# Recurrence hops of a hybrid RWKV/attention layer: the decayed old state is added on VectorE, the output products follow the next hop's first ones, and one woven product changes its place

## Chip, cores, metric

One core of a Trainium2 chip. The metric is the device time of one execution in microseconds, in three runs 1148.97 to 1151.8, median 1151.46. The engines: TensorE (PE in the profile; PEld are its weight loads), VectorE (DVE), ScalarE (ACT), GpSimd (POOL) and SyncE (SP, which issues transfers).

## What is computed

One layer of a diffusion backbone for 512 image tokens and 128 context tokens, 1024 wide: a bidirectional RWKV-7 recurrence (8 heads of 64) beside a neighbourhood attention, then a gated merge and a feed-forward part. The change concerns the recurrence. For every head and direction a 64x64 state s is carried over the tokens:

```python
def _wkv_step(s, inp):
    r, w, k, v, a, b = inp
    sa = jnp.einsum("bhvk,bhk->bhv", s, a)
    s = s * w[:, :, None, :] + sa[..., None] * b[:, :, None, :] + v[..., None] * k[:, :, None, :]
    return s, jnp.einsum("bhvk,bhk->bhv", s, r)

def _wkv_scan(s0, r, w, k, v, a, b, reverse):
    xs = tuple(jnp.moveaxis(t.astype(jnp.float32), 1, 0) for t in (r, w, k, v, a, b))
    s, ys = lax.scan(_wkv_step, s0.astype(jnp.float32), xs, reverse=reverse)
    return s, jnp.moveaxis(ys, 0, 1)
```

The scan runs forwards and backwards, and both outputs are added. Everything is fp32.

## The kernel before

The kernel does the scan in chunks of 64 tokens: eight chunks of image tokens (slots 0 to 7) and two of context tokens (slots 8 and 9). Inside a chunk all products are batched; only the state passes from chunk to chunk. Heads go in pairs: four rounds (`ct` 0 to 3), each with two heads `h`, head 0 in partitions 0 to 63 and head 1 in 64 to 127. A round has three parts: `main` builds a chunk's matrices, `inv` inverts its triangular ones (on VectorE), and `carry` passes the state along. Then the next round follows.

`carry` (from L1368) is a chain of eight hops `s`. In each hop both directions `d` and both heads go one chunk on, so a group of products is four matmuls of 64x64, or eight in hops 0 and 1, where the context chunks join. `ZV[:, l, h, :]` holds for a chunk `l` the state and the values, `Dt` the chunk's decay. A hop has three stages, each ended by a `yield`:

- A: the AG products (L1393) multiply the state; ScalarE copies them out as `x0` (L1396). Meanwhile TensorE does the identity products (L1405), which put a copy of the old state into the PSUM tile `pn`, and the R products (L1411), the state's own share of the output `Y`.
- B: the Rt products (L1420) on `x0`; ScalarE copies them into `ZV` (L1426, twice), over the old state.
- C: the TG0 products (L1433) are added to `pn`; VectorE multiplies `pn` by the decay into the next chunk's `ZV` (L1445, one instruction for each head, both directions at once). TensorE goes on with the TG1 products (L1450), the output's share of this hop. In hop 1 a copy of the context outputs ends the stage (L1453).

So the chain of a hop is: AG, copy, Rt, copies, TG0, update, next AG. TensorE would stand idle during every copy and update. `weave` fills these holes: at each `yield` it takes an entry of the plan `PRM["plan"]`, two numbers in the hops. The first says how many feature products from another part of the kernel (L223, 128x320 outputs in PSUM tiles `fl`) are put there, the second how many steps of the next round's preparation are taken (through `beside`, L1586 and below). "0.0 8.1 6.2" is one hop: none in stage A, eight in stage B, six in stage C. The `fl` tiles have two PSUM buffers. The first product of a new one waits for the engine that reads the tile before the last: ScalarE, or in round 3 VectorE (L1554, then L1556 on its result).

TensorE, VectorE, ScalarE and GpSimd execute their instructions in the order in which the schedule writes them. What stands behind a waiting instruction waits too. In round 3 VectorE also has L1579, for attention, in pairs between its other work. From round to round L552, L554, L742, L728 and L751 (the next round's preparation) and L1168 follow on VectorE; L1189 is the first product of the next `main`.

Of the kernel before, what the change touches and what calls it, by code (L numbers as in the profile page):

```python
# [7 lines left out]
F32 = mybir.dt.float32  # L8
F32R = mybir.dt.float32r
AF = mybir.ActivationFunctionType  # L10
ALU = mybir.AluOpType
# [3 lines left out]
P = 128  # L15
# [18 lines left out]
         "5.0.0 24.0.0 20.0.0 10.0.0 8.0.0 8.0.0 0.0.0"),  # L34
        ("10.0 1.0 12.1 0.2 0.0 8.1 6.2 0.0 8.1 6.2 0.0 8.1 12.2 0.0 8.1 6.2 0.0 8.1 6.2 0.0 7.1 5.2 "
         "0.0 9.1 6.2 6.0"),
        "22.0 2.0 2.0 2.0",
        ("0.0.0 0.0.0 2.0.1 10.0.0 1.0.0 2.1.1 2.1.1 2.1.1 2.1.1 1.1.1 10.0.0 3.1.0 2.0.0 2.0.0 2.0.0 "
         "2.1.0 2.1.0 10.0.0 2.1.0 2.1.0 2.1.0 2.1.0 2.1.0 2.1.0 12.0.0 2.0.0 2.0.0 2.0.0 2.0.0 2.0.0 "
         "5.0.0 24.0.0 20.0.0 10.0.0 8.0.0 8.0.0 0.0.0"),  # L40
        ("10.0 0.0 8.1 6.2 0.0 8.1 6.2 0.0 8.1 6.2 0.0 8.1 6.2 0.0 8.1 6.2 0.0 7.1 6.2 0.0 8.1 6.2 0.0 "
         "8.1 6.2 6.0"),
        "22.0 2.0 0.0 5.0",
        ("0.0.0 10.0.0 2.0.1 10.0.0 2.0.0 2.1.1 2.1.1 2.1.2 2.1.1 2.1.0 10.0.0 2.0.0 2.0.0 2.0.0 2.1.0 "
         "2.1.0 2.1.0 10.0.0 2.1.0 2.1.0 2.1.0 3.1.0 4.1.0 2.1.0 2.0.0 2.0.0 2.0.0 4.0.0 2.0.0 2.0.0 "
         "5.0.0 24.0.0 18.0.0 8.0.0 9.0.0 8.0.0 0.0.0"),
        ("10.0 0.0 8.1 14.2 0.0 8.1 6.2 0.0 8.1 6.2 0.0 0.1 6.2 0.0 8.1 6.2 0.0 8.1 6.2 0.0 8.1 6.2 "
         "0.0 8.1 6.2 6.0"),
        "27.2 0.0 0.0 5.0",
        ("0.0.0 16.1.0 8.1.1 9.0.0 2.1.0 8.1.1 13.1.1 0.1.1 0.1.1 0.1.1 0.1.0 6.1.0 6.1.0 6.1.0 6.1.0 "  # L50
         "6.1.0 6.1.0 7.1.0 6.0.0 6.0.0 6.0.0 6.0.0 6.0.0 6.0.0 7.0.0 6.0.0 6.0.0 6.0.0 6.0.0 6.0.0 "
         "6.0.0 6.0.0 11.0.0 8.0.0 8.0.0 2.0.0 0.0.0"),
        ("10.3 0.0 6.1 4.2 0.0 6.1 4.2 0.0 6.1 4.2 0.0 6.1 4.2 0.0 6.1 4.2 0.0 6.1 4.2 0.0 6.1 4.2 0.0 "
         "6.1 8.2 6.0"),
# [60 lines left out]
def body(ctx: ExitStack, tc: tile.TileContext, xs, xp, cols, consts, w_ada, b_row, w_rw, w_qkv,  # L115
# [26 lines left out]
    def nm(s):  # L142
        cn[0] += 1
        return f"{s}_{cn[0]}"
# [952 lines left out]
    with ExitStack() as s3:  # L1097
# [270 lines left out]
        def carry(ct, S, last):  # L1368
# [4 lines left out]
            Y = [wps(), wps()]  # L1373
            begun = []

# [10 lines left out]
            for s in range(8):  # L1386
# [4 lines left out]
                for g, (sl, d, l) in enumerate(items):  # L1391
                    for h in range(2):
                        pe.matmul(px[hrows[h], g * 64:g * 64 + 64], AG[:, l, h, :], ZV[:, l, h, :],  # L1393
                                  start=True, stop=True)
                x0 = sb.tile([P, 4, 64], F32, tag="x0", bufs=2, name=nm("x0"))
                act.copy(x0[:, :ng, :], V(px[:, :], [[64, ng], [1, 64]]))  # L1396
                todo = [(g, i) for g, i in enumerate(items) if i[0] != 7]
                if todo:

                    pn = wps()  # L1400
                    for g, (sl, d, l) in todo:
                        for h in range(2):
                            if sl != 8:
                                own = hrows[h]
                                pe.matmul(pn[own, g * 64:g * 64 + 64], idh(h), ZV[own, l, h, :],  # L1405
                                          start=once(pn, h), stop=False)
                for (sl, d, l) in items:
                    for h in range(2):
                        own = hrows[h]
                        if sl != 8:  # L1410
                            pe.matmul(V(Y[sl // 8][own, :], *ycol(sl, d)), ZV[own, l, h, :], R_[own, l, :],  # L1411
                                      start=once(Y[sl // 8], h), stop=False)
                if s == 7 and not PRM["lh"][ct]:
                    last()
# [20 lines left out]
                for g, (sl, d, l) in todo:  # L1435
                    if d == 0:
                        dl = line(sl, 1) - l
                        if sl == 9:
                            dve.tensor_tensor(out=zf, in0=V(pn[:, :], [[64, 2], [1, 64]], 64 * g),
                                              in1=V(Dt[:, 0, :], [[dl, 2], [0, 64]], l), op=ALU.mult)  # L1440
                            sp.dma_start(o_st[ct], zf)
                            continue
                        for h in range(2):
                            own = hrows[h]
                            dve.tensor_tensor(out=V(ZV[own, l + 1, h, :], [[128 * dl, 2], [1, 64]]),  # L1445
                                              in0=V(pn[own, :], [[64, 2], [1, 64]], 64 * g),
                                              in1=V(Dt[own, 0, :], [[dl, 2], [0, 64]], l), op=ALU.mult)
                for (sl, d, l) in items:
                    for h in range(2):
                        pe.matmul(V(Y[sl // 8][hrows[h], :], *ycol(sl, d)), ZV[:, l, h, :], TG[:, l, h, 1, :],  # L1450
                                  start=once(Y[sl // 8], h), stop=sl in (7, 9) and d == 1)
                if s == 1:
                    act.copy(y[:, 512:640], Y[1][:, 0:128])  # L1453
                yield
# [698 lines left out]
```

## Time and profile before

| | before |
|---|---|
| three runs, us | 1151.8, 1148.97, 1151.46 |
| median | 1151.46 |
| the profiled execution | 1151.04 |
| its span | 1149.3 |
| granted TensorE clock, mean | 0.995 |
| the four `carry` parts, from first to last hop, us | 43.84, 44.10, 43.20, 31.60 |

The profiled execution's time is 1.7 us longer than its span; that much lies before the first and behind the last instruction recorded. In rows of the profile a line such as L1445 is a line of the kernel, `out<-in` names what is written and read, `128x64` are partitions and elements, and "x8" counts records. An fp32 matmul leaves two records, so "x8" are four matmuls. Times in a timeline are microseconds from the span's start. Waits are given as "idle before, and what ended it". A view by windows gives for each stretch its length and how long each engine was busy in it.

### The profile page before, as it was taken

Reading aid. Unit: us, or ns where it says so; the run is one execution under the profiler, and the core shown is the slowest. Engines: PE = TensorE matmul, PEld = TensorE weight load, DVE = VectorE, ACT = ScalarE, POOL = GpSimd, SP = SyncE. Lnnn points to the kernel's source line nnn. Section 1 sums busy time; section 2 is a strip of 40 time slices with the busy share of each in tenths; the row PEclk is TensorE's granted clock in tenths of the full one; section 3 lists DMA queues with packets and bytes.
Section 4 is the critical chain, followed back from the end, with each engine's and each line's share of the span. In section 5 each row is a group of like instructions: output and inputs, shape, how many; then the busy total and the mean of one; then the engine's idle time right before and its main releaser. Section 6 shows DMA issues by size and latency. Waiting matters only on the chain.

```text
span 1149.3 us, 26860 instructions
## 1 busy us (share of the span) xinstructions
PE 1117.0 (97%) x11160; PEld 990.9 (86%) x11160; DVE 777.8 (68%) x1641; ACT 533.7 (46%) x1052; POOL 195.1 (17%) x262
## 2 busy tenths in 40 slices
PE   6999999999999999999999999999999999999998
PEld 4688878799888888888898788999899989998997
DVE  4565465769558847936787846897478747874775
ACT  4444576665465665456443524654134413441340
POOL 1163244321101212120100421110101010101000
PEclk8999999999999999999999999999999999999999
DMA  9752677654433533343743872222212221232122
GB/s 340 261 113 91 199 277 236 198 153 125 107 75 86 148 85 93 96 119 86 254 122 105 265 213 72 92 93 93 91 56 92 94 90 55 92 97 88 55 91 94
DMA packets 60482, 149.16 MB, mean 130 GB/s; under 512 B 7460, under 2 KB 22436, under 8 KB 60360
## 3 DMA queue, kind: packets, MB, share of 16 engines
q1 hardware_dynamic: 54888, 131.16, 34.7%
q0 software_dynamic: 4032, 14.68, 6.5%
q10 hardware_dynamic: 1440, 1.59, 0.5%
q8 instruction: 88, 1.44, 0.5%
q14 instruction: 34, 0.28, 0.1%
HBM read 118.41 MB, written 14.32 MB: 115 GB/s over the span
## 4 chain that ended last, share of the span: by engine, by line
PE 74%; DVE 10%; issue 8%; ACT 4%; DMA 2%; POOL 1%; SPq 0%; ACTq 0%; DVEq 0%; POOLq 0%
PE acc L311 24%; PE f L1856 21%; PE fl L223 8%; PE mm L223 5%; PE psa L1044 1%; PE lg L959 1%; PE pt L988 1%; DVE RL L1321 1%; DVE pr L1317 1%; PE po L1006 1%; PE w L1420 1%; PE w L1393 1%; DMA o<-o_d 1%; PE w L1433 1%; DMA wlo<-wst 1%
## 5 line engine op out<-in xcount | busy, mean ns | idle before, releaser
L1856 PE MATMUL f<-t,whi 128*128 128x320 f32 x640 | 141.7, 310 | 0.2
L311 PE MATMUL acc<-whi,u 128*128 128x512 f32 (+1 forms) x448 | 136.1, 386 | 0.0
L1856 PE MATMUL f<-b,whi 128*128 128x320 f32 x608 | 135.0, 310 | 0.4 <-DVE b L212 0.4
L223 PE MATMUL fl<-h,whi 128*128 128x320 f32 x672 | 121.4, 321 | 0.0
L1856 PEld LDWEIGHTS f<-t,whi 128*128 128x128 f32 x640 | 106.8, 188 | 0.8 <-issue 0.4
L223 PEld LDWEIGHTS fl<-h,whi 128*128 128x128 f32 x672 | 102.1, 189 | 4.6
L192 ACT CAST whi<-wst 128x1024 fp32r<-128x1024 f32 (+1 forms) x77 | 79.3, 1033 | 52.2 <-PE acc L311 41.5
L1856 PEld LDWEIGHTS f<-b,whi 128*128 128x128 f32 x608 | 101.7, 188 | 1.1 <-issue 0.6
L1856 PE MATMUL f<-t,wlo 128*128 128x320 f32 x320 | 98.9, 309 | 0.0
L311 PEld LDWEIGHTS acc<-whi,u 128*128 128x128 f32 x448 | 83.5, 188 | 16.6
L1856 PE MATMUL f<-b,wlo 128*128 128x320 f32 x304 | 94.1, 309 | 0.0
L1909 ACT CAST whi<-ws 128x1024 fp32r<-128x1024 f32 x40 | 42.0, 1051 | 104.5 <-PE f L1856 45.6
L311 PE MATMUL acc<-wlo,u 128*128 128x512 f32 (+1 forms) x224 | 86.3, 385 | 0.0
L1923 POOL TENSOR_TENSOR ws<-wst 128x512 f32<-128x512 f32 x20 | 29.1, 1454 | 334.7 <-DVE wlo L1912 226.3
L195 DVE TENSOR_TENSOR wlo<-wst,whi 128x1024 fp32r<-128x1024 f32 (+2 forms) x57 | 60.1, 1066 | 30.6 <-ACT whi L192 30.0
L311 PE MATMUL acc<-whi,h 128*128 128x512 f32 x240 | 79.2, 404 | 0.8 <-DVE h L436 0.8
L1724 DVE SCALAR_TENSOR_TENSOR tt<-acc,G 128x512 f32<-128x512 f32 (+1 forms) x51 | 34.7, 680 | 59.0 <-PE acc L311 45.4
L223 PE MATMUL fl<-h,wlo 128*128 128x320 f32 x336 | 63.8, 322 | 0.0
L1909 ACT CAST whi<-wst 128x1024 fp32r<-128x1024 f32 (+1 forms) x48 | 41.3, 869 | 42.3 <-PE acc L311 25.1
L1856 PEld LDWEIGHTS f<-t,wlo 128*128 128x128 f32 x320 | 60.1, 188 | 0.0
L1912 DVE TENSOR_TENSOR wlo<-ws,whi 128x1024 fp32r<-128x1024 f32 x40 | 55.4, 1386 | 5.4 <-ACT whi L1909 5.4
L1445 DVE TENSOR_TENSOR ZV<-w,Dt 64x128 f32<-64x128 f32 x64 | 18.4, 288 | 58.5 <-PE w L1433 57.4
(342 smaller groups left out, 2533.2 us busy)
## 6 DMA issues: line engine op xcount, KB each, us to landing
wst<-in_w_dram SPq DMA_DIRECT2D x66, 512.0 KB
wst<-in_w_rw_dram SPq DMA_DIRECT2D x31, 512.0 KB
wlo<-wst POOLq DMA_DIRECT2D x28, 512.0 KB, 4.7
wa<-in_w_ada_dram SPq DMA_DIRECT2D x24, 512.0 KB
f<-in_w_ada_dram SPq DMA_DIRECT2D x16, 512.0 KB
wst<-in_w_qkv_dram SPq DMA_DIRECT2D x12, 512.0 KB
o<-o_d SPq DMA_DIRECT2D x14, 320.0 KB
x<-in_xs_dram SPq DMA_DIRECT2D x8, 512.0 KB
```

The source lines that it names most:

```text
L192: act.copy(hi[:, :n], st[:, :n])
L195: dve.tensor_tensor(out=lo[:, a:b], in0=st[:, a:b], in1=hi[:, a:b].bitcast(F32), op=ALU.subtract)
L223: pe.matmul(ps[:, :t1 - t0], w[:, a:a + 128], x[:, k0 + kt, t0:t1], start=n == 0, stop=n == 3 * nk - 1)
L311: pe.matmul(pss[i][:, a:b], lhs(x, kt, ts_), w[:, cs_], start=ki == 0 and n == 0, stop=ki == last and n == 2)
L959: pe.matmul(psl[:, hd, o_:o_ + n], qT[ft][rows, qs], x[rows, :], start=True, stop=True)
L988: pe.transpose(pst[:, c * 128:(c + 1) * 128], L[:, c * 128:(c + 1) * 128], ident)
L1445: dve.tensor_tensor(out=V(ZV[own, l + 1, h, :], [[128 * dl, 2], [1, 64]]), in0=V(pn[own, :], [[64, 2], [1, 64]], 64 * g), in1=V(Dt[own, 0, ...
L1724: dve.scalar_tensor_tensor(out=tt, in0=ps[:, a:b], scalar=c, in1=G[:, g, sl], op0=ALU.mult, op1=ALU.mult)
L1856: pe.matmul(ps[:, :H2], w_[:, c_], x_[:, kt, :], start=first and kt + n == 0, stop=last and kt == 3 and n == 2, skip_group_check=more)
L1909: act.copy(r[0][:, :width], src())
L1912: dve.tensor_tensor(out=r[1][:, :width], in0=src(), in1=r[0][:, :width].bitcast(F32), op=ALU.subtract)
L1923: eng_x(PRM["se"][i - 1]).tensor_tensor(out=o_, in0=x, in1=y, op=op)
```

## The change

In each hop that has a successor (slots 0 to 6) the identity products go. In their place VectorE computes `sd`, old state times decay, right behind the update that made this state (`decayed`, two instructions of 64x128 a hop; hop 0's stand behind its R products). The update is then `pn` times decay plus `sd`, for which a scalar from a pointer is needed: four `scalar_tensor_tensor` of 64x64 a hop (direction 0 head 0, direction 0 head 1, direction 1 head 0, direction 1 head 1) in place of two `tensor_tensor` of 64x128. Only slot 9 keeps its identity products. The TG1 products of a hop are written behind the AG products of the next (`ysum(back)`), those of hop 7 at its end; the copy of the context outputs goes to hop 2 with them. `x0` has one buffer for two. In the plan most hops have one product less in stage B and one more in stage C; the other numbers of the table are unchanged. The rows of rounds 0 and 3 before and after (rounds 1 and 2 are changed alike):

```diff
-        ("10.0 1.0 12.1 0.2 0.0 8.1 6.2 0.0 8.1 6.2 0.0 8.1 12.2 0.0 8.1 6.2 0.0 8.1 6.2 0.0 7.1 5.2 "
-         "0.0 9.1 6.2 6.0"),
+        ("10.0 1.0 11.1 1.2 0.0 7.1 7.2 0.0 7.1 7.2 0.0 8.1 12.2 0.0 7.1 7.2 0.0 7.1 7.2 0.0 6.1 6.2 "
+         "0.0 8.1 7.2 6.0"),
...
-        ("10.3 0.0 6.1 4.2 0.0 6.1 4.2 0.0 6.1 4.2 0.0 6.1 4.2 0.0 6.1 4.2 0.0 6.1 4.2 0.0 6.1 4.2 0.0 "
+        ("10.3 0.0 5.1 5.2 0.0 5.1 5.2 0.0 5.1 5.2 0.0 5.1 5.2 0.0 5.1 5.2 0.0 5.1 5.2 0.0 5.1 5.2 0.0 "
          "6.1 8.2 6.0"),
@@ -1371,7 +1371,22 @@
             S.y = y = out_t()
             zf = sb.tile([P, 2, 64], F32, tag="zf", bufs=1, name=nm("zf"))
             Y = [wps(), wps()]
-            begun = []
+            sd = sb.tile([P, 2, 64], F32, tag="sd", bufs=1, name=nm("sd"))
+            begun, back = [], []
+
+            def decayed(l):
+
+                for h in range(2):
+                    own = hrows[h]
+                    dve.tensor_tensor(out=sd[own, :, :], in0=V(ZV[own, l, h, :], [[128 * 12, 2], [1, 64]]),
+                                      in1=V(Dt[own, 0, :], [[12, 2], [0, 64]], l), op=ALU.mult)
+
+            def ysum(items):
+
+                for (sl, d, l) in items:
+                    for h in range(2):
+                        pe.matmul(V(Y[sl // 8][hrows[h], :], *ycol(sl, d)), ZV[:, l, h, :], TG[:, l, h, 1, :],
+                                  start=once(Y[sl // 8], h), stop=sl in (7, 9) and d == 1)
 
             def once(t, h):
                 first = not any(b is t and i == h for b, i in begun)
@@ -1392,15 +1407,19 @@
                     for h in range(2):
                         pe.matmul(px[hrows[h], g * 64:g * 64 + 64], AG[:, l, h, :], ZV[:, l, h, :],
                                   start=True, stop=True)
-                x0 = sb.tile([P, 4, 64], F32, tag="x0", bufs=2, name=nm("x0"))
+                x0 = sb.tile([P, 4, 64], F32, tag="x0", bufs=1, name=nm("x0"))
                 act.copy(x0[:, :ng, :], V(px[:, :], [[64, ng], [1, 64]]))
+                if back:
+                    ysum(back)
+                    if s == 2:
+                        act.copy(y[:, 512:640], Y[1][:, 0:128])
                 todo = [(g, i) for g, i in enumerate(items) if i[0] != 7]
                 if todo:
 
                     pn = wps()
                     for g, (sl, d, l) in todo:
                         for h in range(2):
-                            if sl != 8:
+                            if sl == 9:
                                 own = hrows[h]
                                 pe.matmul(pn[own, g * 64:g * 64 + 64], idh(h), ZV[own, l, h, :],
                                           start=once(pn, h), stop=False)
@@ -1410,6 +1429,8 @@
                         if sl != 8:
                             pe.matmul(V(Y[sl // 8][own, :], *ycol(sl, d)), ZV[own, l, h, :], R_[own, l, :],
                                       start=once(Y[sl // 8], h), stop=False)
+                if s == 0:
+                    decayed(0)
                 if s == 7 and not PRM["lh"][ct]:
                     last()
                 yield
@@ -1440,17 +1461,26 @@
                                               in1=V(Dt[:, 0, :], [[dl, 2], [0, 64]], l), op=ALU.mult)
                             sp.dma_start(o_st[ct], zf)
                             continue
+                        if sl < 8:
+                            for e in range(2):
+                                for h in range(2):
+                                    own = hrows[h]
+                                    dve.scalar_tensor_tensor(
+                                        out=ZV[own, l + 12 * e + 1, h, :],
+                                        in0=pn[own, (g + e) * 64:(g + e) * 64 + 64],
+                                        scalar=V(Dt[own, 0, :], [[1, 1]], l + 12 * e),
+                                        in1=sd[own, e, :], op0=ALU.mult, op1=ALU.add)
+                            continue
                         for h in range(2):
                             own = hrows[h]
                             dve.tensor_tensor(out=V(ZV[own, l + 1, h, :], [[128 * dl, 2], [1, 64]]),
                                               in0=V(pn[own, :], [[64, 2], [1, 64]], 64 * g),
                                               in1=V(Dt[own, 0, :], [[dl, 2], [0, 64]], l), op=ALU.mult)
-                for (sl, d, l) in items:
-                    for h in range(2):
-                        pe.matmul(V(Y[sl // 8][hrows[h], :], *ycol(sl, d)), ZV[:, l, h, :], TG[:, l, h, 1, :],
-                                  start=once(Y[sl // 8], h), stop=sl in (7, 9) and d == 1)
-                if s == 1:
-                    act.copy(y[:, 512:640], Y[1][:, 0:128])
+                if s < 6:
+                    decayed(s + 1)
+                back = items
+                if s == 7:
+                    ysum(items)
                 yield
             act.copy(y[:, 0:512], Y[0][:, 0:512])
```

In the changed kernel the lines have other numbers: AG L1408, TG1 L1388, R L1430, Rt L1441, TG0 L1454, `sd` L1381, the update L1468 (the context chunks' L1476), L1584 and L1586 for L1554 and L1556, L1609 for L1579.

TensorE in round 1, the last hop but one, from its AG products to those of hop 7, before (w are PSUM tiles, h the features that the woven products multiply; a bracket names the engines waited for):

```order
L1393 MATMUL w_5772<-ZV,AG 64x64 [waits DVE_49] x2
L1393 MATMUL w_5772<-ZV,AG 64x64 x2
L1405 MATMUL w_5779<-ZV,K 64x64 [waits PE_49]
L1405 MATMUL w_5779<-ZV,K 64x64 x3
L1411 MATMUL w_5320<-R__2901,ZV 64x64 x4
L1420 MATMUL w_5788<-x_836_5777,Rt 64x64 [waits Activation_49]
...
L1433 MATMUL w_5779<-ZV,TG 64x64 [waits Activation_49] x2
L1433 MATMUL w_5779<-ZV,TG 64x64 x2
L1450 MATMUL w_5320<-TG,ZV 64x64 x4
L223 MATMUL fl_5744<-h_90,wlo_5368 128x320 x2
L223 MATMUL fl_5744<-h_91,wlo_5368 128x320 x2
L223 MATMUL fl_5744<-h_92,wlo_5368 128x320 x2
```

and in the changed kernel:

```order
L1408 MATMUL w_5772<-ZV,AG 64x64 [waits DVE_49] x4
L1388 MATMUL w_5321<-TG,ZV 64x64 x4
L1430 MATMUL w_5321<-R__2901,ZV 64x64 x4
L1441 MATMUL w_5788<-x_838_5777,Rt 64x64 [waits Activation_49]
...
L1454 MATMUL w_5783<-ZV,TG 64x64 [waits Activation_49] x2
L1454 MATMUL w_5783<-ZV,TG 64x64 x2
L223 MATMUL fl_5744<-h_89,wlo_5394 128x320
L223 MATMUL fl_5744<-h_90,wlo_5394 128x320 x2
L223 MATMUL fl_5744<-h_91,wlo_5394 128x320 x2
L223 MATMUL fl_5744<-h_92,wlo_5394 128x320 x2
```

The identity products are gone, the output products of the hop before stand in their place, seven woven products instead of six lie behind TG0, and each AG product has a wait for VectorE of its own.

VectorE in round 3, hops 3 and 4, before (mx, mt: the reading of a feature tile; P, kk, bv, mt: L1579's tiles):

```order
L1445 TENSOR_TENSOR ZV<-w_8666,Dt_6879 64x2x64 x2
L1554 SCALAR_TENSOR_TENSOR mx_8293<-mx_8293,fl_8628 128x320
L1556 TENSOR_TENSOR mt_7728<-mt_7728,mx_8293 128x320
L1579 SCALAR_TENSOR_TENSOR P_1069_8133<-pre_8633,P_1069_8133 128x320 x2
L1554 SCALAR_TENSOR_TENSOR mx_8653<-mx_8653,fl_8683 128x320
L1556 TENSOR_TENSOR mt_7932<-mt_7932,mx_8653 128x320
L1445 TENSOR_TENSOR ZV<-w_8718,Dt_6879 64x2x64 x2
L1579 SCALAR_TENSOR_TENSOR kk_8283<-pre_8655,kk_8283 128x320 x2
```

and in the changed kernel:

```order
L1468 SCALAR_TENSOR_TENSOR ZV<-w_8672,Dt_6880,sd_8443 64x64 x4
L1381 TENSOR_TENSOR sd_8443<-ZV,Dt_6880 64x128 x2
L1584 SCALAR_TENSOR_TENSOR mx_8296<-mx_8296,fl_8630 128x320
L1586 TENSOR_TENSOR mt_7731<-mt_7731,mx_8296 128x320
L1609 SCALAR_TENSOR_TENSOR P_1072_8136<-pre_8634,P_1072_8136 128x320 x2
L1609 SCALAR_TENSOR_TENSOR kk_8286<-pre_8657,kk_8286 128x320 x2
L1468 SCALAR_TENSOR_TENSOR ZV<-w_8724,Dt_6880,sd_8443 64x64 x4
L1381 TENSOR_TENSOR sd_8443<-ZV,Dt_6880 64x128 x2
L1584 SCALAR_TENSOR_TENSOR mx_8655<-mx_8655,fl_8685 128x320
L1586 TENSOR_TENSOR mt_7935<-mt_7935,mx_8655 128x320
```

The reading of the second feature tile (fl_8683, now fl_8685) stood ahead of hop 4's update and stands behind it and behind the two `sd`; the pair for kk came ahead of it.

TensorE at the end of the same hop 4, before:

```order
L1433 MATMUL w_8718<-ZV,TG 64x64 [waits Activation_49] x2
L1433 MATMUL w_8718<-ZV,TG 64x64 x2
L1450 MATMUL w_8438<-TG,ZV 64x64 x4
L223 MATMUL fl_8734<-o_7943,wlo_8296 128x320 x2
L223 MATMUL fl_8734<-o_7944,wlo_8296 128x320
L223 MATMUL fl_8756<-o_7943,whi_8597 128x320 [waits DVE_49]
L1393 MATMUL w_8764<-ZV,AG 64x64 [waits DVE_49] x2
```

and in the changed kernel:

```order
L1454 MATMUL w_8724<-ZV,TG 64x64 [waits Activation_49] x2
L1454 MATMUL w_8724<-ZV,TG 64x64 x2
L223 MATMUL fl_8736<-o_7950,whi_8298 128x320
L223 MATMUL fl_8736<-o_7946,wlo_8299 128x320 x2
L223 MATMUL fl_8736<-o_7947,wlo_8299 128x320
L223 MATMUL fl_8758<-o_7946,whi_8594 128x320 [waits DVE_49]
L1408 MATMUL w_8766<-ZV,AG 64x64 [waits PE_49]
```

In both the last woven product ahead of AG is the first of a new feature tile and waits for VectorE's reading of the tile before the last, fl_8683 or fl_8685; what moved is that reading, on VectorE, as shown above.

More of the change, by code (lines that the diff above doesn't have):

```diff
@@ L40 @@
          "5.0.0 24.0.0 20.0.0 10.0.0 8.0.0 8.0.0 0.0.0"),
-        ("10.0 0.0 8.1 6.2 0.0 8.1 6.2 0.0 8.1 6.2 0.0 8.1 6.2 0.0 8.1 6.2 0.0 7.1 6.2 0.0 8.1 6.2 0.0 "
-         "8.1 6.2 6.0"),
+        ("10.0 0.0 7.1 7.2 0.0 7.1 7.2 0.0 7.1 7.2 0.0 7.1 7.2 0.0 7.1 7.2 0.0 6.1 7.2 0.0 7.1 7.2 0.0 "
+         "7.1 7.2 6.0"),
         "22.0 2.0 0.0 5.0",
@@ L46 @@
          "5.0.0 24.0.0 18.0.0 8.0.0 9.0.0 8.0.0 0.0.0"),
-        ("10.0 0.0 8.1 14.2 0.0 8.1 6.2 0.0 8.1 6.2 0.0 0.1 6.2 0.0 8.1 6.2 0.0 8.1 6.2 0.0 8.1 6.2 "
-         "0.0 8.1 6.2 6.0"),
+        ("10.0 0.0 8.1 14.2 0.0 7.1 7.2 0.0 7.1 7.2 0.0 0.1 6.2 0.0 7.1 7.2 0.0 7.1 7.2 0.0 7.1 7.2 "
+         "0.0 7.1 7.2 6.0"),
         "27.2 0.0 0.0 5.0",
```

## The prediction

> **What bounds the kernel now.** First the page's busy times, then the windows of the four rounds of the recurrence, then the timeline of one hop on TensorE and VectorE, then the chain of waits where one round passes into the next.
>
> ```profile
> PE 1117.0 (97%) x11160; PEld 990.9 (86%) x11160; DVE 777.8 (68%) x1641; ACT 533.7 (46%) x1052; POOL 195.1 (17%) x262
> ```
>
> TensorE (PE) is busy for 97% of the span, so an instruction taken from it is worth its time wherever nothing else ends later. VectorE (DVE) has 32% to spare on average, but averages hide stages. The windows (length, then busy time of PE, PEld, DVE, ACT, POOL) are rounds 0 to 3 from their first to their last hop, the stretch behind round 3, and the single hops 1, 2, 3, 4 and 5 of round 3, cut at the start of the state update:
>
> ```profile
> 298.86:342.70 43.84, 42.19 (x595) 36.64 (x595) 17.68 (x36) 28.09 (x72) 5.34 (x9) 1.00 0.32 78
> 393.90:438.00 44.10, 42.56 (x598) 37.01 (x597) 22.07 (x42) 27.60 (x72) 7.69 (x11) 1.00 0.30 83
> 492.20:535.40 43.20, 42.08 (x593) 36.85 (x593) 17.35 (x35) 25.87 (x70) 5.91 (x9) 1.00 0.38 99
> 598.40:630.00 31.60, 31.56 (x528) 26.83 (x527) 20.69 (x50) 10.95 (x35) 0.00 (x0) 1.00 0.40 120
> 630.00:720.00 90.00, 87.28 (x454) 72.90 (x453) 59.32 (x112) 39.09 (x71) 25.88 (x26) 1.00 0.59 180
> 607.41:611.13 3.72, 3.72 (x65) 3.13 (x60) 2.39 (x7) 2.01 (x6) 0.00 (x0) 1.00 0.15 45
> 611.13:614.85 3.72, 3.72 (x66) 3.13 (x60) 3.16 (x9) 0.79 (x3) 0.00 (x0) 1.00 0.69 204
> 614.85:618.57 3.72, 3.72 (x66) 3.13 (x60) 3.25 (x9) 0.79 (x3) 0.00 (x0) 1.00 0.48 146
> 618.57:622.29 3.72, 3.72 (x66) 3.13 (x60) 3.25 (x9) 1.62 (x4) 0.00 (x0) 1.00 0.05 19
> 622.29:626.01 3.72, 3.72 (x66) 3.13 (x60) 2.52 (x6) 0.79 (x3) 0.00 (x0) 1.00 0.62 165
> ```
>
> Rounds 0 to 2 leave TensorE idle 1.65, 1.54 and 1.12 us, 4.3 together; round 3 leaves it 0.04, and behind it 2.7 of 90 us. So what round 3 gains or loses passes to the end almost whole. In its hops TensorE is full and VectorE has only 0.47 to 1.33 us left of 3.72. That is the place to look. Hop 2's update and what TensorE does next, then VectorE in the same stretch (start, length of the group):
>
> ```profile
> 612.03 0.45 PE L1393 MATMUL w<-ZV,AG 128*64 128x64 f32 x8
> 612.41 0.45 PE L1405 MATMUL w<-ZV,K 64*64 64x64 f32 x8
> 612.69 0.40 PE L1411 MATMUL w<-R__2901,ZV 64*64 64x64 f32 x8
> 612.92 0.42 PE L1420 MATMUL w<-x,Rt 64*64 64x64 f32 x8
> 613.28 0.41 PE L223 MATMUL fl<-o,wlo 128*128 128x320 f32 x1
> ...
> 614.35 0.45 PE L1433 MATMUL w<-ZV,TG 128*64 128x64 f32 x8
> 614.63 0.40 PE L1450 MATMUL w<-TG,ZV 128*64 128x64 f32 x8
> 614.96 0.41 PE L223 MATMUL fl<-o,whi 128*128 128x320 f32 x1
> ...
> 615.75 0.28 PE L1393 MATMUL w<-ZV,AG 128*64 128x64 f32 x2
> ```
>
> ```profile
> 611.13 0.61 DVE L1445 TENSOR_TENSOR ZV<-w,Dt 64x128 f32<-64x128 f32 x2 [0.37 <-PE w L1433]
> 611.77 0.49 DVE L1554 SCALAR_TENSOR_TENSOR mx<-mx,fl 128x320 f32<-128x320 f32 x1
> ...
> 612.70 0.89 DVE L1579 SCALAR_TENSOR_TENSOR mt<-pre,mt 128x320 f32<-128x320 f32 x2
> 613.50 0.89 DVE L1579 SCALAR_TENSOR_TENSOR P<-pre,P 128x320 f32<-128x320 f32 x2
> 614.85 0.28 DVE L1445 TENSOR_TENSOR ZV<-w,Dt 64x128 f32<-64x128 f32 x1 [0.46 <-PE w L1433]
> ```
>
> Read off: the update (L1445) starts 0.50 us after the TG0 products (L1433, 614.35 to 614.85) and takes 0.61 for its pair; the AG products of the next hop follow at 615.75, 0.90 after the update's start, so the update is hidden by 0.29. Four woven products with the change of tile shape behind them take 0.79 (614.96 to 615.75), six 1.07 (613.28 to 614.35): 0.14 each, and 0.23 for the change.
>
> **The identity products removed.** From AG to R is 0.66 us with the identity group (612.03 to 612.69). In hop 7, which has none, it is 0.38:
>
> ```profile
> 530.59 0.45 PE L1393 MATMUL w<-ZV,AG 128*64 128x64 f32 x8
> 530.97 0.33 PE L1411 MATMUL w<-R__2901,ZV 64*64 64x64 f32 x4
> ```
>
> So a group costs at most 0.28, and at least the 0.23 of an equal group (R, 612.69 to 612.92). I take 0.25, 21 groups in rounds 0 to 2: -5.25 us. Hop 0 of rounds 1 and 2 weaves nothing ahead of Rt, and with no earlier products to move there the wait for the x0 copy takes the group's place: +0.5. Of the 4.3 us of idle TensorE in these rounds I count six waits for ACT's copies: what is saved ahead of such a wait is waited, 6 x 0.25 = +1.5.
>
> **The output products moved.** They go from behind TG0 to behind AG: the same instructions, so nothing by themselves. There they do for the x0 copy what the identity products did. But they leave the place where they covered the state update, and one woven product (0.14) is put there for 0.28 to 0.33 taken away.
>
> **The four pointer-scalar updates.** The trace has no such instruction of 64x64. Its neighbours:
>
> ```profile
> L684 DVE SCALAR_TENSOR_TENSOR kk<-kt__626,C,w x3: 340/340/342, 313.9 to 511.1; 128x128 f32<-128x128 f32 x3
> L682 DVE SCALAR_TENSOR_TENSOR kk<-kt__626,C,w x3: 746/746/747, 313.3 to 510.4; 128x512 f32<-128x512 f32 x3
> L1310 DVE SCALAR_TENSOR_TENSOR RL<-RL x24: 234/241/251, 284.1 to 585.9; 128x28 f32<-128x28 f32 x12, 128x29 f32<-128x29 f32 x8, 128x30 f32<-128x30 f32 x4
> L1445 DVE TENSOR_TENSOR ZV<-w,Dt 64x128 f32<-64x128 f32 x64 | 18.4, 288 | 58.5 <-PE w L1433 57.4
> ```
>
> From 512 to 128 columns it falls by 406 ns, 1.06 a column; 64 columns fewer than L684 gives 0.27. Bounds: 0.22 (L1445 less 64 columns) and 0.34 (L684 unchanged); 28 columns at 0.24 speak for the middle, so 0.28. L1445's pair, which changes between the partition halves, takes 0.61 for 2 x 0.288, while the L1579 pairs, which stay in one place, overlap (0.89 for 2 x 0.49). The new ones alternate halves each time: 0.31 apart, 1.24 for four, 0.63 more than now.
>
> [...]
>
> Consequence where seven products are now woven behind TG0: TensorE reaches AG 0.28 + 0.05 + 7 x 0.14 + 0.23 = 1.54 after TG0. The fourth update is ready at 0.50 + 1.24 + 0.05 = 1.79, and the fourth AG product starts some 0.2 after the first, so AG may start at 1.59. A wait of 0.05 if VectorE is free at that moment, 0.29 with updates of 0.34 (0.37 apart); with 0.28 between them, and pieces of 0.8 us of VectorE's own work that may be in front, I take 0.13 for some 15 such hops: +2.0 (0 to 4.4). With five woven (round 3) it is 1.26 against 1.59: AG now hangs on VectorE.
>
> **Where the update ends last already.** Chain of waits, rounds 0 to 1 and end of round 2:
>
> ```profile
> 336.89 0.28 DVE ZV L1445
> ...
> 337.54 0.76 DVE vp L552
> ...
> 344.17 0.73 DVE AG L1168
> ...
> 347.50 0.54 PE w L1189 x34
> ```
>
> ```profile
> 530.03 0.84 DVE f L742
> ...
> 530.96 0.65 ACT NK L721
> 531.61 0.16 ACT x L1396
> ...
> 531.81 0.45 PE w L1420 x8
> ```
>
> From the last update on VectorE works without a gap worth naming to the next round's first products; in round 2 L742 stands behind hop 6's update, and ACT's L721 and x0 copy, and with them Rt, wait for it. In each the update is 0.6 longer; I count three (the change from round 1 to 2 looks the same): +1.8.
>
> Rounds 0 to 2: -5.25 + 0.5 + 1.5 + 2.0 + 1.8 = +0.55.
>
> **The decayed state.** Two tensor-tensors of L1445's form a hop, 0.65 with their gaps, right behind the update in VectorE's written order: VectorE has 0.63 + 0.65 = 1.28 us more a hop. In rounds 0 to 2 it has 22 us or more idle of 43, and it is hidden (if not, up to 0.65 x 18 = 12 us; nothing there waits for sd itself but the next update and the copies over the old state, both over 1 us later). In round 3 the windows say otherwise: hop 2 has 3.16 + 1.28 = 4.44 against 3.72, +0.72. Hop 3 loses L1554 and L1556 (two of 0.49) to hop 4 and takes the kk pair (0.89) from it: about 3.25 - 0.98 + 0.89 + 1.28 = 4.44, +0.72. Hop 1 with 2.39 + 1.28 = 3.67 stays inside. TensorE's own hop is then AG at 1.59 and from AG to TG0 2.32 - 0.28 + 0.28 - 0.14 = 2.18, 3.77 together: +0.05 for each of hops 1, 5 and 6; hop 5's VectorE has 2.52 + 1.28 = 3.80, +0.1 with it; hop 0 has six updates, +0.1.
>
> **A wait that the new order makes.** In hop 4 of round 3 the last woven product ahead of AG opens a feature buffer and waits for the L1554 of the buffer two before. That stood ahead of hop 4's update; now it stands behind the four updates and the two decays, and the AG, output and R products of hop 5 are queued behind the waiting product on TensorE. From the update's start: 1.24 + 0.65 + 0.49 (L1554) + 0.05 + 0.14 + 0.23 = 2.80 to AG, where it was 0.90: +1.90, less 0.14 by which AG to the next update gets shorter (2.68 for 2.82): +1.76.
>
> Round 3: 0.72 + 0.72 + 1.76 + 0.3 = +3.5. The rest (one x0 buffer, whose reader is done a hop earlier; the output copy behind x0; L650 and L660 in other places of ACT's order) I put at 0 with 0.5 either way. The sum: 0.55 + 3.5 = +4.05, which is 1155.1 from the profiled execution's 1151.04; that lies 0.4 under the median 1151.46, so **1155.5** against the median.
>
> **Rivals.**
> *The chip hides VectorE's part.* If an update is 0.22 and the alternating ones overlap, so that four end within 0.9, the AG waits vanish, rounds pass at +0.3 and only TensorE's saving counts: 28 x 0.25 = -7.0, + 0.5 + 1.5 + 0.9 = -4.1, hop 4's wait shrunk into hops with room: 1147.4. For it: PE 97%. Against: L1445's pair does not overlap.
> *Gain and loss cancel.* At 0.22, 0.25 apart, four take 1.0: no wait in rounds 0 to 2 (-2.0), three passages +0.4 instead of 0.6 (-0.6), three late hops 0.24 shorter (-0.7): +0.75, 1152.2.
> *VectorE becomes the bound, at L684's price.* 0.34, 0.37 apart, 1.48 for four: 0.24 more on every hop, 15 x 0.24 + 3 x 0.24 + 6 x 0.24 = +5.8: about 1161. It decides from 0.31 on, where AG waits in rounds 0 to 2 as well. Against it: fewer columns than L684.
> That the change doesn't do what it says can be left out: the built order shows 112 products gone and the new updates in place.
>
> **How the numbers follow.** The forecast 0.52, its own range 1152.5 to 1158; hidden 0.20; cancelled 0.10; VectorE's bound 0.18. A measurement here tells 0.3%, 3.45 us, from none: faster is under 1148.0, slower over 1154.9. The forecast lies close to that edge, two thirds of it above: slower 0.18 + 0.34 = 0.52, same 0.10 + 0.18 = 0.28, faster 0.20. The range 1148 to 1160 leaves out the better half of the first rival and the worse half of the last.
>
> **What would show it.** Right: updates of 0.27 to 0.29, 0.31 apart; hops 2 and 3 of round 3 near 4.4 with TensorE waiting for VectorE ahead of AG; the hop 4 to 5 passage 1.5 to 2 us longer, with a woven product waiting there for the read that was L1554; rounds 0 to 2 within 1 us of before. Wrong: updates under 0.25 or overlapping, round 3's hops still 3.7, or rounds 0 to 2 shorter by 3 us and more, which would mean that TensorE's saving was not eaten by ACT.

## The result and the profile after

The changed kernel takes 1163.24 us in the median of six runs (1161.16 to 1165.57), the kernel before 1151.12 (six runs): a ratio of 1.011 with an interval of 1.0093 to 1.0127, slower by 12 us. The forecast was 1155.5 with a range up to 1160. It was right that the change makes the kernel slower; the size was wrong.

First the page's own lines for the changed kernel: busy times, and TensorE's instruction fetches (packets, MB, share of the DMA engines).

```profile
PE 1120.7 (96%) x10936; PEld 991.2 (85%) x10936; DVE 810.0 (70%) x1753; ACT 534.9 (46%) x1052; POOL 194.1 (17%) x262
...
q8 instruction: 86, 1.41, 0.5%
```

There are 224 TensorE records fewer (112 products), and TensorE is still busy for 3.7 us longer. So work was taken away and what is left takes longer. The starts of the AG products tell where: each round's first and its hop 7, read from the timelines of both kernels.

| stretch | before, us | after, us | difference |
|---|---|---|---|
| up to round 0 | 298.86 | 296.94 | -1.9 |
| hops of round 0 | 38.37 | 37.96 | -0.4 |
| between rounds 0 and 1 | 56.99 | 62.39 | +5.4 |
| hops of round 1 | 38.97 | 36.29 | -2.7 |
| between 1 and 2 | 59.17 | 58.94 | -0.2 |
| hops of round 2 | 38.23 | 39.17 | +0.9 |
| between 2 and 3 | 67.90 | 73.61 | +5.7 |
| hops of round 3 | 28.42 | 33.60 | +5.2 |
| the rest | 522.3 | 522.6 | +0.3 |

Round 3's hops lose 5.2 us where 3.5 were foretold. But 11 us lie between the rounds, in `main` and `inv`, which the change doesn't touch; round 1's hops, which start 3 us late, give some of it back. The windows of the two long stretches, before and then after (length, busy PE, PEld, DVE, ACT, POOL, then the granted clock):

```profile
337.20:394.20 57.00, 55.32 (x1082) 51.11 (x1082) 52.56 (x161) 33.35 (x66) 11.55 (x22) 1.00 0.44 112
...
530.60:598.50 67.90, 64.68 (x1149) 59.88 (x1148) 54.71 (x164) 33.40 (x68) 7.34 (x13) 1.00 0.50 166
```

```profile
334.90:397.30 62.40, 58.26 (x1092) 53.38 (x1092) 54.87 (x166) 33.34 (x66) 11.58 (x22) 0.97 0.41 105
...
531.70:605.30 73.60, 68.09 (x1155) 62.94 (x1155) 55.57 (x165) 33.52 (x68) 7.28 (x13) 0.95 0.47 153
```

The instructions are the same but for a handful, ACT and POOL are busy for as long. TensorE idles 4.1 and 5.5 us where it idled 1.7 and 3.2, and its clock is below 1.00. What it waits for in the whole kernel, by the view of waits (us in total, times, longest), before and after:

```profile
PE w L1208 <- issue: 1.5, 1, 1.5
...
PE w L1359 <- issue: 1.3, 1, 1.3
...
PE w L1259 <- issue: 0.4, 1, 0.4
...
PE w L1211 <- issue: 0.4, 1, 0.4
```

```profile
PE w L1211 <- issue: 4.1, 2, 2.6
PE fl L223 <- DVE mx L1584: 3.6, 3, 2.2
...
PE w L1359 <- issue: 1.4, 2, 0.7
...
PE w L1208 <- issue: 1.0, 1, 1.0
...
PE w L1189 <- issue: 0.6, 1, 0.6
```

"issue" is idle time for which the profile knows no releaser. It was 3.6 us, it is 7.3 (with one of 0.2 not shown). The longest, on TensorE's timeline, and the clock around it in windows of 2 us:

```profile
568.43 0.28 PE L1211 MATMUL w<-R__2901,f 64*64 64x64 f32 x3
571.29 0.21 PE L1211 MATMUL w<-R__2901,f 64*64 64x64 f32 x1 [2.58 <-issue]
```

```profile
568.00:570.00 2.00, 0.71 (x37) 0.58 (x28) 0.36 (x3) 0.00 (x0) 0.00 (x0) 1.00 0.26 95
570.00:572.00 2.00, 0.71 (x14) 0.61 (x14) 0.00 (x0) 0.00 (x0) 0.00 (x0) 1.00 0.02 3
572.00:574.00 2.00, 2.00 (x8) 1.77 (x7) 1.34 (x6) 0.78 (x2) 0.28 (x1) 0.55 0.03 8
574.00:576.00 2.00, 2.00 (x8) 1.61 (x8) 1.94 (x7) 0.15 (x1) 0.59 (x1) 0.59 0.00 0
576.00:578.00 2.00, 2.00 (x16) 2.00 (x15) 1.96 (x6) 0.74 (x2) 0.93 (x1) 1.00 0.42 159
```

In the middle of a burst of products of one kind TensorE stands for 2.58 us, all engines have next to nothing to do, and then the clock is at half for 3.4 us (in the trace's clock record from 572.21 to 575.62 us). In the kernel before, the same burst runs through. What differs is the instruction stream: the queue q8 of the page moves 1.44 MB in 88 packets before, 16 KB each, for 2 x 11160 TensorE records, about 64 bytes a record. A packet is thus 256 instructions, and one 64x64 fp32 product (two records and two weight loads) is four. Such a packet is called a block here. From 560 us to the end of the jam of data transfers (the queue's lines, before up to 566.5 us; after, 568.5 to 571.3):

```profile
q1 hardware_dynamic: 1243, 2.39, 96.9%
q8 instruction: 2, 0.03, 1.9%
```

```profile
q1 hardware_dynamic: 32, 0.06, 6.9%
q8 instruction: 1, 0.02, 2.2%
```

Before, two blocks are fetched while the data transfers have the DMA engines full. In the changed kernel the same view from 560 to 568.4 us lists no fetch at all; the next one lies within the stall (from 568.87 to 569.87 us). This gave the theory for the experiments (**fetch**): by 28 products a round, 112 instructions, the ends of the blocks move against the bursts of small products, and a block that ends in the wrong place is there too late. The rivals: the losses come from what the change does to other engines or to the order of loads (**work**); or they are chance.

Round 3, VectorE (hops 2 to 4) and TensorE (hop 4 to 5) in the changed kernel:

```profile
618.53 1.23 DVE L1468 SCALAR_TENSOR_TENSOR ZV<-w,Dt,sd 64x64 f32<-64x64 f32 x4 [0.20 <-PE w L1454]
619.79 0.61 DVE L1381 TENSOR_TENSOR sd<-ZV,Dt 64x128 f32<-64x128 f32 x2
...
622.96 1.22 DVE L1468 SCALAR_TENSOR_TENSOR ZV<-w,Dt,sd 64x64 f32<-64x64 f32 x4
...
627.39 1.19 DVE L1468 SCALAR_TENSOR_TENSOR ZV<-w,Dt,sd 64x64 f32<-64x64 f32 x4
628.61 0.61 DVE L1381 TENSOR_TENSOR sd<-ZV,Dt 64x128 f32<-64x128 f32 x2
629.25 0.49 DVE L1584 SCALAR_TENSOR_TENSOR mx<-mx,fl 128x320 f32<-128x320 f32 x1
```

```profile
629.79 0.41 PE L223 MATMUL fl<-o,whi 128*128 128x320 f32 x1 [2.23 <-DVE mx L1584]
630.13 0.65 PE L1408 MATMUL w<-ZV,AG 128*64 128x64 f32 x8
...
633.77 0.45 PE L1454 MATMUL w<-ZV,TG 128*64 128x64 f32 x8
```

VectorE goes from update to update in 4.43 us, with no pause of 0.15 us or more (618.53, 622.96, 627.39); the woven product of hop 4 waits 2.23 us for L1584; AG follows 2.74 us after the update's start. All that stood in the prediction. What did not: from AG to TG0 hop 5 takes 3.64 us (630.13 to 633.77) where 2.2 were foretold, at half clock (in the clock record from 630.24 to 633.65 us).

### The profile page after: what moved, and what is told of

Its sections match the earlier page's. It is cut to its first block, busy times and chain, and to the rows that moved or that the text cites. A ratio compares the mean times of both kernels' runs of the same rounds, so it can differ in the third digit from the quotient of the medians.

```text
span 1161.6 us, 26547 instructions
## 1 busy us (share of the span) xinstructions
PE 1120.7 (96%) x10936; PEld 991.2 (85%) x10936; DVE 810.0 (70%) x1753; ACT 534.9 (46%) x1052; POOL 194.1 (17%) x262
## 3 DMA queue, kind: packets, MB, share of 16 engines
q10 hardware_dynamic: 1440, 1.59, 0.5%
## 4 chain that ended last, share of the span: by engine, by line
PE 71%; DVE 11%; issue 9%; ACT 5%; DMA 3%; POOL 1%; SPq 0%; DVEq 0%; ACTq 0%; POOLq 0%
PE acc L311 24%; PE f L1886 21%; PE fl L223 9%; PE mm L223 5%; DVE RL L1321 1%; DVE pr L1317 1%; PE pt L988 1%; PE lg L959 1%; PE po L1006 1%; PE psa L1044 1%; DMA wa<-in_w_ada_dram 1%; PE w L1441 1%; DMA wlo<-wst 1%; PE w L1454 1%; PE w L1408 1%
## 5 line engine op out<-in xcount | busy, mean ns | idle before, releaser
L311 PE MATMUL acc<-whi,u 128*128 128x512 f32 (+1 forms) x448 | 136.0, 385 | 0.0
L311 PEld LDWEIGHTS acc<-whi,u 128*128 128x128 f32 x448 | 83.5, 188 | 16.7
L311 PE MATMUL acc<-wlo,u 128*128 128x512 f32 (+1 forms) x224 | 86.3, 385 | 0.0
L311 PE MATMUL acc<-whi,h 128*128 128x512 f32 x240 | 79.2, 404 | 0.4 <-DVE h L436 0.4
L1468 DVE SCALAR_TENSOR_TENSOR ZV<-w,Dt,sd 64x64 f32<-64x64 f32 x112 | 31.7, 283 | 42.9 <-PE w L1454 40.1
```

Of the source, the lines that this page charges most:

```text
L311: pe.matmul(pss[i][:, a:b], lhs(x, kt, ts_), w[:, cs_], start=ki == 0 and n == 0, stop=ki == last and n == 2)
L1468: dve.scalar_tensor_tensor(out=ZV[own, l + 12 * e + 1, h, :], in0=pn[own, (g + e) * 64:(g + e) * 64 + 64], scalar=V(Dt[own, 0, :], [[1, 1] ...
```

## The experiments

All are timed beside runs of the kernel before on the same chip (medians 1151 to 1152).

**More products, other place of the block ends.** At 16 us, where TensorE has pauses, idle products are put in, whose result is overwritten:

```diff
             ps = pp.tile([P, 512], F32, tag="tp", name=nm("xt"))
+            if i == 3 and q == 0:
+                for _ in range(N):
+                    pe.matmul(ps[0:64, 0:64], ident[0:64, 0:64], ident[0:64, 0:64], start=True, stop=True)
```

with N = 20 in the changed kernel, and 44, 64, 16 and 32 in the kernel before.

> The changed kernel with 20 idle TensorE products of 64x64 (80 instructions) put into TensorE's pause at 17 us, so that the stream up to round 3 is again as long as before's, counted modulo 256 instructions. Theory (fetch): the 2.58 us stall of TensorE at 568.7 us, for which the trace names no engine, is a block of 256 instructions fetched too late in a burst of small products; with the other phase it goes, and the half clock behind it too: 1163.2 - 2.6 - 1.5 = about 1159. Rival (work): the stall comes from what the change does to the other engines or to the order of the loads, and stays where it is: 1163 within 1.5.

> The kernel before with 44 such idle products (176 instructions, which is -80 modulo 256), so that it has the phase of the changed kernel at the start of round 3. Theory (fetch): a stall of 2 to 3 us appears near the L1211 products behind round 3's start, with 3.4 us of half clock behind it: 1151.1 + 4 = about 1155. Rival (work): no stall there, 1151 to 1152.5 (44 products cost at most 2.4 us if none of it is hidden).

> The kernel before with 64 idle TensorE products (256 instructions, one whole 16 KB block) at the place where 44 of them (176 instructions) gave 1163.5 us. Theory (fetch): only the place of the block ends counts; with a whole block every later block ends where it did before, so the stalls go again: 1151 to 1154 (64 products cost at most 3.5 us if none of it is hidden). Rival (work): idle products cost by themselves or by what they delay at the start: at least as much as 44 did, 1163 or more.

> The kernel before with 16 idle products (64 instructions, a quarter of a block). Theory (fetch): some phase between 0 (1151.3) and 176 (1163.5); the burst behind round 0 stalls as soon as its block ends later than its small products begin: anywhere from 1150 to 1163, with the sum of TensorE's unnamed stalls in the trace moving with the time. Rival (work, 16 products cost under 1 us): 1151 to 1152.

> The kernel before with 32 idle products (128 instructions, half a block). Theory (fetch): as with 16, another phase, 1151 to 1163, again with the unnamed stalls; were it a smooth cost of added work, it would lie between the times with 16 and 44.

| kernel | instructions added | modulo 256 | median, us | ratio to before | unnamed stalls of TensorE, us | half clock, us |
|---|---|---|---|---|---|---|
| before | 0 | 0 | 1151 | | 3.6 | 3.4 |
| pad_before16 | 64 | 64 | 1168.14 | 1.0144 (1.0124 to 1.0163) | 6.7 | 23.9 |
| pad_before32 | 128 | 128 | 1165.73 | 1.0111 (1.0087 to 1.0136) | 13.8 | 17.1 |
| pad_before | 176 | 176 | 1163.52 | 1.0111 (1.0096 to 1.0126) | 10.1 | 3.4 |
| pad_before64 | 256 | 0 | 1153.79 | 1.0018 (1.0006 to 1.0029) | 3.5 | 0 |

(The stalls are the sum of the lines "PE ... <- issue" of each profile; half clock is its time between 100 and 1140 us in the trace's clock record.) Sixteen idle products, which take TensorE 2.1 us in the trace, cost 17 us in a kernel that is otherwise unchanged; 64 of them, which take 7.7, cost 2.5 (that is 0.12 to 0.13 a product, where my expectations had 0.06). So it is not the work but the place modulo one block. The view of waits with 44 products, where L1214 is the line that was L1211:

```profile
PE w L1214 <- issue: 8.4, 6, 2.4
...
PE w L1262 <- issue: 1.7, 1, 1.7
```

With 44 the stretch between rounds 0 and 1 is 5.3 us longer, as in the changed kernel (5.4), though no instruction of the recurrence was edited, and the foretold stall is there: 2.37 us at 572.40, among the products where the changed kernel had 2.58.

The traces allow a direct count. Over all records of TensorE (products, weight loads and the sequencer's own, 22508 before) the 14 traces of the runs here have 75 unnamed stalls of 0.15 us or more, of 0.16 to 3.73. Every one of them begins behind a number of records that is 193 modulo 256 (the 2.58 us behind 14017), in the kernel before and move_only too. And each ends 1.2 to 1.6 us after a packet of q8 has landed, which in all 75 has the same number as the block: behind 256n + 193 records it is the n-th packet (the 54th ahead of the 2.58 us). A stall caused by other engines or by the order of loads would have no reason to keep to that count. So what TensorE waits for there is its next block of instructions.

So the theory holds in its main point. In its details my expectations missed: with 44 products 1155 was expected and 1163.5 came, with 16 at most 1163 and 1168 came; and pad_after, which should have come to 1159 because round 3 has before's phase again, took 1168.06 (1.0141, 1.0127 to 1.0155). There the stretch between rounds 2 and 3 does fall from +5.7 to +1.0 us against before, but the parts ahead of round 0 and behind round 3 got +6.0 and +2.7 (in the changed kernel -1.9 and +0.3). One pad can't set all the bursts, since the change moves each round's by another amount. How late a block will be I can't foretell; only that the same number of instructions modulo 256 gave nearly the same time (64 products here, and the last experiment). Is the sum of stalls alone the cost? With 16 products it grows by 3.1 us and the time by 17: 20 us more of half clock come behind, which by estimate cost half of that (three records of L587 that follow each other in 0.43 us before take 0.80 in r3_only at half clock), and later transfers (in that trace TensorE waits 3.6 us for one load of L311 that cost 0.6 before). With 44 there is no more half clock than before, the stalls make 6.5 of the 12 us, and the rest was not taken apart.

**The same number of instructions.** In the changed kernel the identity products are kept, into columns that nobody reads:

```diff
-                            if sl == 9:
+                            if sl != 8:
                                 own = hrows[h]
-                                pe.matmul(pn[own, g * 64:g * 64 + 64], idh(h), ZV[own, l, h, :],
+                                c = g * 64 + (256 if sl < 8 else 0)
+                                pe.matmul(pn[own, c:c + 64], idh(h), ZV[own, l, h, :],
```

> The changed kernel with the identity products kept as idle ones (in a part of the PSUM tile that nobody reads): all the work of the change plus the TensorE time that it was to save, but before's number of TensorE instructions at every place. Theory (fetch): the 11 us lost outside the recurrence's hops go (+5.4 ahead of round 1, +5.7 ahead of round 3), up to 7 us of TensorE time come back: 1154 to 1160, faster than the changed kernel although it does more. Rival (work): 1163 to 1170.

1160.18 us (1.0074, 1.0057 to 1.0091): 3 us faster than the changed kernel (1.011) with 112 products more. Its unnamed stalls are 2.7 us. The stretch between rounds 0 and 1 is +0.4 to before, for +5.4; between 2 and 3 +2.1, for +5.7. Its hops of round 3 lose 7.1 us, more than the changed kernel's 5.2, as TensorE has the idle products there as well. So with before's block ends most of the loss is in round 3.

**The change by rounds.** Each `if` of the change gets the round as a second condition, with the plan's rows to match; r012 has it in rounds 0 to 2, r3_only in round 3.

```diff
-                            if sl == 9:
+                            if sl == 9 or (ct in (0, 1, 2) and sl != 8):
...
-                if s < 6:
+                if s < 6 and ct not in (0, 1, 2):
                     decayed(s + 1)
```

> The change in rounds 0 to 2 alone; round 3 has the identity products, the two-headed update, the output products in their old place and its old row of the plan. If round 3's carry costs what the trace shows (5.2 us): 1163.2 - 5.2 = 1158.0, with TensorE's stall near 569 us still there, and 1152 plus what rounds 0 to 2 cost (about 1) if the stall is not a lasting part of the kernel. If the loss in round 3 came only from the lateness that it was handed: 1162.

> The change in round 3 alone; rounds 0 to 2 as before, so that the blocks lie as before up to round 3. Round 3's hops lose the 5.2 us that the changed kernel's trace shows there, nothing else: 1156.5 (1155 to 1158). If the stalls ahead of round 3 belong to what the change does in round 3: 1161 or more.

r3_only: 1156.66 (1.0042, 1.0026 to 1.0058), as foretold; its hops of round 3 are 4.24, 5.74, 4.05, 3.95, 6.84, 4.96 and 3.52 us, the changed kernel's to within 0.3. r012: 1160.13 (1.0084, 1.0068 to 1.01), 2 us above what I had expected; its round 3 has before's hops of 3.72 again, its rounds 0 to 2 the stretch +5.7 ahead of round 1 and +3.2 ahead of round 3. So rounds 0 to 2, where TensorE saves work and VectorE has room, cost 9 us alone. That the parts' 9.0 and 5.4 are more than the whole's 12.1 fits a cost that depends on the block ends of each kernel, but was not taken apart further.

**Round 3: the wait and what stands behind it.** r3_plan puts back round 3's row of the plan (its first diff lines, read backwards), by which L1584 stands ahead of hop 4's update.

> The changed kernel with only round 3's row of the plan as before (6.1 4.2 for 5.1 5.2): by this the reading of the second feature tile stands ahead of hop 4's update again. Theory (order): the wait of the last woven product in hop 4 goes (2.2 us) and the half clock behind it in hop 5 (1.2 us); the hop falls from 6.84 to about 4.4: about 1159.5. Rival (load): VectorE's 1.28 us more a hop are the cause, the lateness only moves to another hop: round 3 keeps its 5 us, 1162 to 1163.

1162.09 us (1.0101, 1.0088 to 1.0115). The wait of 2.23 is gone from its trace, no half clock follows, but round 3 is still 3.4 us longer than before (for 5.2): its hops 2 to 6 are 4.19, 4.10, 4.55, 4.55 and 4.30. The rival was more right, and it puts the bound in VectorE's queue itself. To see which of its two additions, the next kernel has the change in round 3 only, the old row, and `decayed` on GpSimd:

```diff
-                    dve.tensor_tensor(out=sd[own, :, :], in0=V(ZV[own, l, h, :], [[128 * 12, 2], [1, 64]]),
+                    pool.tensor_tensor(out=sd[own, :, :], in0=V(ZV[own, l, h, :], [[128 * 12, 2], [1, 64]]),
```

> The change in round 3 alone, with its plan row as before (so that the feature tile is read ahead of hop 4's update) and the decayed state computed by GpSimd instead of VectorE, which in round 3's hops has nothing to do. Theory (VectorE's queue): VectorE keeps 0.63 us more a hop in place of 1.28, which fits into 3.72; round 3's hops fall from 4.05 to 6.84 (change) and 4.1 to 4.55 (row alone) to 3.8 to 4.0: round 3 costs 1 us or less, 1152. Rival (the four updates are the cost, or GpSimd is too slow for the next update): hops stay at 4.1 or more, 1154.5 and above.

1154.91 us (1.0036, 1.0025 to 1.0048): hops of 4.28, 4.14, 4.06, 4.05 and 4.17, round 3 +2.5. Less, but not down to 3.8: the updates bind too.

```profile
617.14 0.45 PE L1454 MATMUL w<-ZV,TG 128*64 128x64 f32 x8
617.53 0.42 PE L223 MATMUL fl<-o,whi 128*128 128x320 f32 x1
617.78 0.60 PE L223 MATMUL fl<-o,wlo 128*128 128x320 f32 x3
618.31 0.97 PE L1408 MATMUL w<-ZV,AG 128*64 128x64 f32 x7
```

```profile
617.72 1.23 DVE L1468 SCALAR_TENSOR_TENSOR ZV<-w,Dt,sd 64x64 f32<-64x64 f32 x4 [0.17 <-PE w L1454]
```

AG starts as soon as TensorE is there (618.31) but spreads over 0.97 us, for 0.45 before, because its fourth product waits for the update that ends at 618.95. So the last test orders the four by head, one change of half in place of three:

```diff
-                            for e in range(2):
-                                for h in range(2):
+                            for h in range(2):
+                                for e in range(2):
```

> As r3_pool, with the four updates of a hop in the order head 0 direction 0, head 0 direction 1, head 1 direction 0, head 1 direction 1, so that the partition half changes once and not three times. Theory (the change of half keeps them from overlapping): inside a half two of them overlap as L1579's pair does (0.09 of 0.49 there), four take 1.05 to 1.15 for 1.23, and round 3's hops fall from 4.05 to 3.9: 1154. Rival (each update costs its 0.28 however it is ordered): 1.23 stays, 1154.9 within 0.7.

```profile
616.55 0.99 DVE L1468 SCALAR_TENSOR_TENSOR ZV<-w,Dt,sd 64x64 f32<-64x64 f32 x4 [0.18 <-PE w L1454]
```

Four take 0.99 us in place of 1.23 (a single one still 0.28), the late hops 3.82, round 3 is +1.1, and the kernel takes 1152.98 us: 1.0006 (0.9994 to 1.0018), no difference from before. The theory's 1.05 to 1.15 was too careful. The same four instructions take 1.23 us with three changes of half and 0.99 with one.

**The move alone**: identity products and old update kept, output products behind the next hop's AG products, the plan as changed (`sl != 8` and the old branch of the update for all rounds).

> Only the move: output products behind the next hop's AG products, one woven product from stage B to C, in all rounds; identity products and the old update stay, so the number of TensorE instructions is before's. Theory (fetch, and VectorE as the cost in round 3): no loss at all, 1150 to 1152; the x0 copy is covered by 0.25 us more, which may take up to 1 us from the waits for it. Rival (the move costs): the update lies 0.14 to 0.2 us barer in 24 hops, 1154 to 1156.

1151.78 us (1.0001, 0.999 to 1.0012): nothing, as expected. The move and the plan are free; the number of TensorE instructions is before's. same_len differs from this kernel by VectorE's added work and by the column that the identity products write, has the same number of TensorE instructions, and takes 8.4 us more, 6.5 of them in the hops of round 3 (35.5 us for 29.0). So VectorE's share of the change, which round 3 has no room for, costs by itself, without any shift of the blocks.

No version beat the kernel before. What the change may gain in rounds 0 to 2 with before's block ends and without the identity products was not tried: the two go together.

## Why the prediction was wrong

**The sizes that it worked out were right.** A pointer-scalar update: 0.28 foretold, 0.284 measured; four of them 1.24 and 1.23; the decayed state 0.65 and 0.64 (618.53 + 1.26 to 620.42 on the timeline). VectorE's steps in hops 2 and 3 of round 3: 4.44 and 4.43. From hop 4's update to AG: 2.80 and 2.74.

```profile
L1468 DVE SCALAR_TENSOR_TENSOR ZV<-w,Dt,sd x112: 249/284/293, 301.5 to 639.0; 64x64 f32<-64x64 f32 x112
```

**Round 3: +3.5 foretold, +5.2 measured** (r3_only +5.4 in time). The term mis-sized is the passage behind the wait: I let AG to the next update shrink by 0.14, but the pause of 2.23 us is followed by half clock, and AG to TG0 takes 3.64 for 2.2, +1.4.

**Rounds 0 to 2: +0.55 foretold; their hops measured -0.4, -2.7 and +0.9.** Of round 1's, hop 0 alone has -2.9 (9.17 to 6.25 us), most of it lateness taken back and ScalarE's new order, which I had put at 0 within 0.5; in same_len, where the round starts on time, the same hop is 1.5 shorter. move_only, which keeps the identity products, has it 1.5 shorter too, so that part is the new order. The waits that I counted are there: in these hops TensorE's idle time for the x0 copy grows from 1.0 to 2.7 us (+1.5 foretold), and the AG groups, which now wait for one update after the other, are about 1.6 us longer from first start to last (+2.0 foretold). So the hops themselves came out near the working, which has -1.25 for them, at -2.2.

**The step that failed** is "the rest [...] I put at 0 with 0.5 either way", and with it the thought that a part of the program which the change doesn't touch keeps its time. The stretches between the rounds cost +5.4, -0.2 and +5.7 us, for which the working had only the +1.8 of the later updates. They have the same instructions but for a handful; these stand at other places of the 16 KB blocks. Sixteen products that do nothing do the same to the kernel before, and worse. Of the 12 us about 5 are the change's own work in round 3. For the rest the runs show the place of the block ends as the cause of the stalls; how much of it each half-clock spell and each later transfer adds was not taken apart. No rival of the prediction had this mechanism. That the forecast said slower was no luck, since round 3 alone makes it so (r3_only); but nothing in it stands for the other half of the loss. The two-sided bounds of 0.5 were taken over instructions that were moved, none over instructions that were merely displaced.

## What to carry to other kernels

A kernel can sit at a lucky place of its own instruction stream: the kernel before lies 12 to 17 us below the same kernel with 16, 32 or 44 idle products. So compare changes to TensorE's instruction count at an equal count modulo 256 (here 256 instructions more cost 2.5 us, 64 more 17), before the difference is put down to the change. Keeping the removed products as idle ones in their places did that here; one pad at the start did not, as the change shifts each round by another amount. And a saving on the busiest engine paid with time on another is to be checked in that stage where the other is nearly full, here 3.2 of 3.72 us, with the instruction behind which the busiest engine's next wait is queued.

## What the runs showed of the hardware

**Instruction blocks.** TensorE's instructions come in packets of 16 KB on a DMA queue of their own (1.44 MB in 88). Between 254 and 603 us, where the small fp32 products are, a block can be late by up to 3.7 us. The nine stalls of 2 us or more all follow 4 us in which data transfers took at least 58% of the DMA engines' time; where they took under 30%, none was over 0.7 us. In the 14 traces the packet of a block starts about when the block before begins (median 0.3 us after it, from 4.8 ahead to 6.2 behind). In the long stall of the changed kernel that block lasted only 3.1 us (565.59 to 568.71), and the packet came 3.3 us after its begin. Behind 620 us, where the products are larger, every block had landed 5.8 us or more before it was needed. Stalls of 2.7 (same_len) to 13.8 us (pad_before32) a kernel lie at the block ends. Whether a late packet was asked for late or served late, no trace here shows.

**Half clock.** A pause is followed by half clock, but not each time. The kernel before and r3_only give TensorE the same instructions up to round 3; in both it waits 1.59 us for L573. Before, the products behind run at full clock, in r3_only (windows of 2 us) they don't:

```profile
547.00:549.00 2.00, 0.74 (x3) 0.74 (x4) 1.03 (x1) 2.00 (x5) 0.00 (x0) 0.88 0.00 0
549.00:551.00 2.00, 2.00 (x9) 2.00 (x9) 1.58 (x3) 0.13 (x1) 0.81 (x6) 0.50 0.35 104
551.00:553.00 2.00, 2.00 (x16) 2.00 (x14) 0.00 (x0) 0.00 (x0) 0.00 (x0) 0.77 0.97 334
```

The stretch between rounds 2 and 3 is 1.5 us longer in r3_only. The changed kernel has such a spell at the same wait (a pause of 1.37 us, half clock from 548.32 to 551.73 us), so some 1.5 of its +5.7 there can't be put down to the change. From 100 to 1140 us each spell in the traces lasts 3.41 or 6.83 us, and the spells of one kernel start whole multiples of 3.413 us apart (in the changed kernel at 353.76, 548.32, 572.21 and 630.24 us, 57, 7 and 17 such steps). A pause of a whole step is not needed, as 1.59 us were enough in r3_only. There the pause (546.67 to 548.26 us) lies whole within one step, counted from the spells' starts. In move_only and r3_pool it does too, and full clock stays, so where it falls does not settle it here.
